# A hybrid decoder layer on one core: seven instead of six of the sixteen contraction pairs in seven block products, and the bias rows stored 32 times per head in the second pass

## The chip, the core and the metric

The kernel runs on one core of one Trainium2 chip. The metric is the device time of one execution, in microseconds (us); a shorter time is better. The engines are TensorE (PE, matmuls; its weight loads are the row PEld), VectorE (DVE), ScalarE (ACT), GpSimd (POOL, idle here) and SyncE (SP), whose queue issues every DMA of this kernel.

## What is computed

The input x has 256 tokens of width 4096. All numbers are float32.

```python
u    = rmsnorm(x, norm_gain)                       # per token
proj = u @ w_in                                    # 4096 x 16384
q, k, v, z_a, hc, b_gate, c_gate, z_c = split(proj, 8)          # 2048 columns each
attn = causal_attention(q, k, v, bias=T5_buckets(rel_bias)) * silu(z_a)   # 16 heads x 128
conv = b_gate * short_conv(c_gate * hc, conv_w) * silu(z_c)     # 3 taps along the tokens
h    = x + concatenate([attn, conv]) @ w_out       # 4096 x 4096
out  = rmsnorm(h, final_gain)
```

With 256 tokens and blocks of 256 the block-sparse attention is plain causal attention within one block. The bias of a query and a key depends on the head and on their distance alone.

## The kernel before, in words

**Passes, quads and units.** The two projections are cut into 20 passes. A pass makes two blocks of 512 output columns for both halves (128 each) of the tokens, so it has four sums of [128, 512]. Passes 0 to 15 are the input projection, passes 16 to 19 the output projection. Passes 0, 2, 4, 6 end in q and k of a group of four heads (`qk_end`), passes 1, 3, 5, 7 in v and z of that group (`vz_end`), passes 8 to 15 in the convolution's inputs (`hc_end`, `zb_end`).

The contraction over 4096 goes in 16 pairs of two tiles of 128. What one pass does with one pair is a quad: one weight load `raw` of [128, 2048] (1 MB), three buffers deep. A quad of an ordinary pair is 8 block products in two units of four. A quad of a pair in `SEVEN` is 7 block products after the Strassen-Winograd pattern, in three units of 3, 2 and 2: they need sums of weight blocks (`sum`, L461 to L463, on DVE) and sums of activation blocks (`c`, `sums_of`, L113), and their products are shared by several of the four outputs. A pass therefore keeps eight PSUM banks, b1 to b8, as accumulators. Banks 1, 5, 6 and 7 belong to the seven products alone and are done with the last `SEVEN` quad of the pass; banks 2, 3, 4 and 8 go on to the end.

A block product is three matmuls of 512 columns (L529, L530, L531): every operand is split into a high part `hi` (a cast on ACT, L472) and the rest `lo` (a subtraction on DVE, L473), and high x high, low x high and high x low are added. `hi` and `lo` have three buffers each, a buffer holding one unit, and `split(u + 2)` stands ahead of the products of unit u. So DVE and ACT can be at most three units ahead of PE. The load of quad n + 2 is issued when the first unit of quad n is split.

**What lies beside it.** In pass 0 the activations are loaded per pair (`xr`, 256 KB), scaled by the gain and split once for all passes: `x_parts`, which for a `SEVEN` pair has 4 sums (L113), a cast of 896 columns (L116) and a subtraction of 896 columns (L117), and else two activations (L137) and two subtractions (L138). Pass 0 also loads x again (`xq`, 8 x 512 KB) for the sum of squares per token (`squares`, L155) and makes the bias rows: a matmul of the table with a one-hot matrix gives one row of 384 values per head, and L195 writes it 128 times per head into DRAM (`bias_d`). A head's bias tile `bt` [128, 384] is read back with a row step of 383 elements, so each partition sees the row one place further on; that takes two DMAs, of 128 KB (L206) and 64 KB (L208). `bias_load(h + 2)` is called in `scores(h)`, after the addition that frees its buffer (L226).

The attention and the convolution are tasks placed among the block products behind the last `SEVEN` quad of a pass (`tasks_of`, L477): `turn`, `scores` and `probs` of four heads in passes 1, 3, 5, 7; `values` and `mixed` in passes 2, 4, 6, 8; `conv` in passes 10, 12, 14 and, from its start, in pass 16. They use banks 1, 5, 6 and 7. `early` (L310) first reads those banks into `e`, with four additions of [128, 512] on DVE; `two_done` (L325) adds the other four banks after the pass's last product. In passes 16 to 19 `out_early` and `out_end` do the same with the residual. In passes 15 and 16 `m_parts` (L146) splits the new operands for the output projection, as `x_parts` does.

**What sets the order.** `ORDERS` gives the pair of each quad of a pass: `FIRST` in pass 0, `OUT_FIRST` in pass 16, and 0, 1, 2, ... in the others. The numbers in `tasks_of` count block products behind the last `SEVEN` quad. The framework then orders each engine's instructions and puts in the waits. SP's queue is in order, and its DMAs report on eight semaphores, DMAHW0 to DMAHW7, in turn, so that a DMA waits until the one eight places before it has landed.

Of the kernel before, what the change touches and what calls it, by code (L numbers as in the profile page):

```python
# [17 lines left out]
P = 128  # L18
# [16 lines left out]
BUCKETS = 32  # L35

# [11 lines left out]
SEVEN = frozenset((0, 2, 4, 6, 8, 10))  # L48
FIRST = (1, 3, 5, 7, 0, 9, 2, 11, 4, 13, 6, 12, 8, 14, 10, 15)
# [10 lines left out]
def hymba_layer(ctx: ExitStack, tc: tile.TileContext, xT, xres, gain, w, convw, wout,  # L60
# [17 lines left out]
    bias_d = dram.tile([H, P, 384], F32, name="bias_d")  # L78
# [76 lines left out]
    def squares(p):  # L155
        for t in range(2):
            xq = pool.tile([P, 2, B], F32, name="xq", tag="vz"[t])
            xq = xq.rearrange("p n c -> p (n c)")
            nc.sync.dma_start(xq, xres[p][:, t * 2 * B:(t + 1) * 2 * B])
            nc.scalar.activation(xq, xq, AF.Square, accum_out=sx[:, t, p:p + 1])  # L160
# [23 lines left out]
    def bias_rows():  # L184
# [10 lines left out]
        nc.sync.dma_start(bias_d, row[:, None, :].to_broadcast([H, P, 384]))  # L195
# [4 lines left out]
    def bias_load(h):  # L200
        if h >= H:
            return
        bt = BT[h] = pool.tile([P, 384], F32, name="bt", bufs=2)

        base = bias_d.offset + h * P * 384
        nc.sync.dma_start(bt[:, :S], bass.AP(tensor=bias_d.tensor, offset=base + 127,  # L206
                                             ap=[[383, P], [1, S]]))
        nc.sync.dma_start(bt[:, S:], bass.AP(tensor=bias_d.tensor, offset=base + 255,  # L208
                                             ap=[[383, P], [1, P]]))
# [125 lines left out]
    def vz_end(g):  # L335
        V[g], Z[g] = (pool.tile([P, 2, B], F32, name=x) for x in "vz")
        two_done((V[g], Z[g]), (rT, rT))
        nc.scalar.activation(Z[g], Z[g], AF.Silu)
# [138 lines left out]
    def tasks_of(p):  # L477
# [5 lines left out]
        if p < 8 and p % 2:  # L483
            for j, (at, banks) in enumerate(zip(((6, 10, 18), (9, 13, 21), (15, 19, 27), (18, 22, 30)),
                                                ((1, 7, 5), (6, 1, 7), (5, 6, 1), (7, 5, 6)))):
                for f, a_, n in zip((turn, scores, probs), at, banks):
                    put(a_, f, p // 2 * HG + j, n)
        elif 2 <= p <= 8:
            for j, (at, banks) in enumerate(zip(((6, 10), (10, 14), (14, 18), (18, 22)),
# [3 lines left out]
        elif p in (10, 12, 14):  # L493
            for j in range(4):
                put(6 + 4 * j, conv, (p - 10) // 2 * 4 + j, (1, 6, 7, 5)[j])
# [38 lines left out]
    for u, (n, kind, at, products) in enumerate(units):  # L534
# [129 lines left out]
```

## Time and profile before

| | |
|---|---|
| median of 3 runs | 1776.4 us (1776.03 to 1777.66) |
| profiled execution, its own time | 1777.55 us |
| its span | 1775.8 us |
| mean granted TensorE clock | 0.989 |
| PE busy | 1723.9 us, 97% of the span, 7698 matmuls |
| DVE busy | 1458.5 us, 82% |
| ACT busy | 1010.4 us, 57% |
| DMA | 370.5 MB, mean 209 GB/s |

All further numbers come from this one execution. Its page gives sums over the whole span; `windows` rows give, for a stretch of time, the busy time of each engine with the count of its instructions in brackets, then the granted clock, the busy share of the DMA engines and GB/s. Rows of groups give the number of instructions, their busy time together, and the mean of one in ns. Neighbouring instructions of DVE overlap a little, so a sum of means is somewhat above the busy time. The times at which passes and quads begin, in us from the start of the span, are the starts of their first matmuls.

### The profile page before, as it was taken

What the parts mean: (1) busy time and instruction counts of PE and PEld (TensorE: products, weight loads), DVE (VectorE), ACT (ScalarE), POOL (GpSimd) and SP (SyncE); (2) the same over time, 40 slices, a digit from 0 to 9 for tenths busy, and PEclk for the clock granted to TensorE, in tenths of its full rate; (3) what the DMA queues carried; (4) which work ended last, traced back from release to release, by engine and by line L of the source; (5) the groups of instructions that cost most, each with busy time, mean ns of one, the idle gap of its engine ahead of it and who ended that gap; (6) DMA issues with size and microseconds to landing.
All of it is one profiled execution on the core that took longest, in us unless ns stands there. A gap on an engine that the chain in (4) does not pass through costs nothing.

```text
span 1775.8 us, 20607 instructions
## 1 busy us (share of the span) xinstructions
PE 1723.9 (97%) x7698; PEld 1414.8 (80%) x7698; DVE 1458.5 (82%) x1591; ACT 1010.4 (57%) x1104; POOL 0.7 (0%) x6
## 2 busy tenths in 40 slices
PE   9489999999999999999999999999999999999996
PEld 7368888888888888888888888888888888788885
DVE  7498787878787878787878887887889999888886
ACT  6375665566556555755555564655555655555553
POOL 0000000000000000000000000000000000000000
PEclk9799999999999999999999999999999999999998
DMA  7875555555555555555645555555555776555563
GB/s 233 233 268 200 206 191 201 191 206 191 200 200 197 199 194 213 174 214 194 223 183 206 203 212 195 213 197 212 194 213 216 260 275 255 201 212 202 193 224 152
DMA packets 65264, 370.53 MB, mean 209 GB/s; under 512 B 7275, under 2 KB 13452, under 8 KB 24460
## 3 DMA queue, kind: packets, MB, share of 16 engines
q1 hardware_dynamic: 65164, 369.22, 58.0%
q8 instruction: 60, 0.98, 0.2%
q14 instruction: 40, 0.33, 0.1%
HBM read 357.66 MB, written 11.53 MB: 208 GB/s over the span
## 4 chain that ended last, share of the span: by engine, by line
PE 93%; DVE 2%; DMA 2%; ACT 1%; issue 1%; SPq 0%; DVEq 0%; ACTq 0%
PE p L531 30%; PE p L529 30%; PE p L530 30%; DMA raw<-in_w_dram 2%; DVE lo L473 1%; ACT hi L472 1%; PE p L216 0%; DMA xq<-in_xres_dram 0%; PE p L223 0%; PE p L240 0%; DVE hg L402 0%; ACT xq L160 0%; DVE hg L414 0%; PE p L251 0%; PE p L250 0%
## 5 line engine op out<-in xcount | busy, mean ns | idle before, releaser
L529 PE MATMUL p<-hi,k 128*128 128x512 f32 x2440 | 958.3, 394 | 32.1 <-ACT hi L472 31.7
L530 PE MATMUL p<-hi,k 128*128 128x512 f32 x2440 | 951.2, 390 | 0.0
L531 PE MATMUL p<-lo,k 128*128 128x512 f32 x2440 | 945.0, 391 | 3.8 <-DVE lo L473 3.3
L473 DVE TENSOR_TENSOR lo<-raw,hi 128x1024 fp32r<-128x1024 f32 (+2 forms) x524 | 692.0, 1333 | 138.5 <-ACT hi L472 137.0
L472 ACT CAST hi<-raw 128x1024 fp32r<-128x1024 f32 (+2 forms) x524 | 596.1, 1145 | 290.3 <-PE p L530 241.9
L529 PEld LDWEIGHTS p<-hi,k 128*128 128x128 f32 x2440 | 459.3, 188 | 132.1 <-ACT hi L472 38.7
L531 PEld LDWEIGHTS p<-lo,k 128*128 128x128 f32 x2440 | 458.2, 188 | 106.5 <-DVE lo L473 9.0
L530 PEld LDWEIGHTS p<-hi,k 128*128 128x128 f32 x2440 | 459.5, 188 | 93.6 <-issue 0.6
L472 ACT CAST hi<-sum 128x1024 fp32r<-128x1024 f32 x240 | 252.9, 1054 | 377.1 <-PE p L530 233.7
L473 DVE TENSOR_TENSOR lo<-sum,hi 128x1024 fp32r<-128x1024 f32 x240 | 292.7, 1219 | 105.7 <-ACT hi L472 105.4
L461 DVE TENSOR_TENSOR sum<-raw 128x1024 f32<-128x1024 f32 x120 | 146.3, 1219 | 6.4 <-DMA raw<-in_w_dram 4.6
L462 DVE TENSOR_TENSOR sum<-sum,raw 128x512 f32<-128x512 f32 x120 | 82.0, 683 | 0.3
L463 DVE TENSOR_TENSOR sum<-sum,raw 128x512 f32<-128x512 f32 x120 | 81.8, 682 | 0.1
L580 ACT ACTIVATE e<-e,rT 128x512 f32<-128x512 f32 x56 | 37.8, 715 | 2.0 <-DVE e L314 1.4
L138 DVE SCALAR_TENSOR_TENSOR k<-xr,g_sb,k 128x256 fp32r<-128x256 f32 x20 | 9.0, 479 | 26.1 <-ACT k L137 26.1
L137 ACT ACTIVATE k<-xr,g_sb 128x256 fp32r<-128x256 f32 x20 | 9.2, 500 | 25.4 <-DMA xr<-in_xT_dram 23.7
L116 ACT CAST k<-c 128x896 fp32r<-128x896 f32 (+1 forms) x22 | 17.3, 796 | 7.9 <-PE p L531 5.0
L117 DVE TENSOR_TENSOR k<-c,k 128x896 fp32r<-128x896 f32 (+1 forms) x22 | 19.7, 902 | 2.4 <-ACT k L116 2.4
L301 DVE SCALAR_TENSOR_TENSOR y<-p,cw,y 128x255 f32<-128x255 f32 (+1 forms) x32 | 15.4, 480 | 4.7 <-ACT y L299 4.3
L226 DVE TENSOR_TENSOR lg<-p,bt 128x384 f32<-128x384 f32 x16 | 8.9, 555 | 12.3 <-PE p L224 12.3
L231 ACT ACTIVATE lg<-lg,st 128x256 f32<-128x256 f32 (+1 forms) x32 | 14.3, 448 | 5.8 <-DVE st L230 5.5
L299 ACT ACTIVATE y<-p,cw 128x256 f32<-128x256 f32 x16 | 7.5, 470 | 12.0 <-PE p L297 12.0
(101 smaller groups left out, 425.5 us busy)
## 6 DMA issues: line engine op xcount, KB each, us to landing
raw<-in_w_dram SPq DMA_DIRECT2D x254, 1024.0 KB, 4.8
raw<-in_wout_dram SPq DMA_DIRECT2D x64, 1024.0 KB, 4.8
xr<-in_xT_dram SPq DMA_DIRECT2D x16, 256.0 KB, 7.8
xq<-in_xres_dram SPq DMA_DIRECT2D x8, 512.0 KB, 6.3
c<-m_d SPq DMA_DIRECT2D x16, 256.0 KB, 3.3
hg<-in_xres_dram SPq DMA_DIRECT2D x4, 1024.0 KB, 7.7
bias_d<-row SPq DMA_DIRECT2D x1, 3072.0 KB, 33.4
out_dram<-hg SPq DMA_DIRECT2D x6, 512.0 KB, 4.0
```

What stands on the lines that cost most here:

```text
L116: nc.scalar.copy(dst[:, :, 0], c)
L117: nc.vector.tensor_tensor(dst[:, :, 1], c, dst[:, :, 0].bitcast(F32), ALU.subtract)
L301: nc.vector.scalar_tensor_tensor(y[:, i:], ps[:, :S - i], cw[:, k, 2 - i:3 - i], y[:, i:], op0=ALU.mult, op1=ALU.add)
L461: nc.vector.tensor_tensor(t[:, :2], raw[:, 1:3], raw[:, :1].to_broadcast([P, 2, B]), ALU.add)
L462: nc.vector.tensor_tensor(t[:, 2], t[:, 0], raw[:, 2], ALU.add)
L463: nc.vector.tensor_tensor(t[:, 3], t[:, 2], raw[:, 3], ALU.add)
L472: nc.scalar.copy(hi[:, c], src[:, c])
L473: nc.vector.tensor_tensor(lo[:, c], src[:, c], hi[:, c].bitcast(F32), ALU.subtract)
L529: nc.tensor.matmul(acc[b_], a, h_, start=s0, stop=False)
L530: nc.tensor.matmul(acc[b_], b, h_, start=False, stop=False)
L531: nc.tensor.matmul(acc[b_], a, l_, start=False, stop=s1)
L580: nc.scalar.activation(es[name], es[name], AF.Copy, scale=rows[c][:, t:t + 1])
```

## The change

Pair 12 joins `SEVEN`. The order of the pairs in pass 0 is another: the first `SEVEN` quad is the third quad, not the fifth. In `OUT_FIRST`, which stays as it was, pair 12 stands between 8 and 10, so that three `SEVEN` quads follow each other. The tasks are placed closer, since only three quads (24 block products) are left behind the last `SEVEN` quad of a usual pass instead of five (40). The bias rows are made in quad 0 of pass 0 instead of quad 2, written 32 instead of 128 times per head, and stored later; a bias tile is then read in eight DMAs (four bands of 32 partitions, 32 KB and 16 KB each) instead of two. The squares take one half-load per quad in quads 4 to 11 instead of two per quad in quads 6 to 9, into other buffers; v and z share buffers with q and k.

```diff
+COPIES = 32
-SEVEN = frozenset((0, 2, 4, 6, 8, 10))
-FIRST = (1, 3, 5, 7, 0, 9, 2, 11, 4, 13, 6, 12, 8, 14, 10, 15)
+SEVEN = frozenset((0, 2, 4, 6, 8, 10, 12))
+FIRST = (1, 3, 0, 5, 2, 7, 4, 9, 6, 11, 8, 13, 10, 14, 12, 15)
...
-    bias_d = dram.tile([H, P, 384], F32, name="bias_d")
+    bias_d = dram.tile([H, COPIES, 384], F32, name="bias_d")
...
-    def squares(p):
-        for t in range(2):
-            xq = pool.tile([P, 2, B], F32, name="xq", tag="vz"[t])
...
+    def squares(n):
+        p, t = divmod(n, 2)
+        xq = pool.tile([P, 2, B], F32, name="xq", tag="qk"[t]).rearrange("p n c -> p (n c)")
+        nc.sync.dma_start(xq, xres[p][:, t * 2 * B:(t + 1) * 2 * B])
+        nc.scalar.activation(xq, xq, AF.Square, accum_out=sx[:, t, p:p + 1])
...
-        nc.sync.dma_start(bias_d, row[:, None, :].to_broadcast([H, P, 384]))
+        return row
+
+    def bias_store(row):
+        nc.sync.dma_start(bias_d, row[:, None, :].to_broadcast([H, COPIES, 384]))
...
-        base = bias_d.offset + h * P * 384
-        nc.sync.dma_start(bt[:, :S], bass.AP(tensor=bias_d.tensor, offset=base + 127,
-                                             ap=[[383, P], [1, S]]))
-        nc.sync.dma_start(bt[:, S:], bass.AP(tensor=bias_d.tensor, offset=base + 255,
-                                             ap=[[383, P], [1, P]]))
+        base = bias_d.offset + h * COPIES * 384
+        for a in range(0, P, COPIES):
+            for c0, c1, at in ((0, S, P - 1), (S, 384, S - 1)):
+                nc.sync.dma_start(bt[a:a + COPIES, c0:c1],
+                                  bass.AP(tensor=bias_d.tensor, offset=base + at - a,
+                                          ap=[[383, COPIES], [1, c1 - c0]]))
...
-        V[g], Z[g] = (pool.tile([P, 2, B], F32, name=x) for x in "vz")
+        V[g], Z[g] = (pool.tile([P, 2, B], F32, name=x, tag=y) for x, y in ("vq", "zk"))
...
-            for j, (at, banks) in enumerate(zip(((6, 10, 18), (9, 13, 21), (15, 19, 27), (18, 22, 30)),
+            for j, (at, banks) in enumerate(zip(((4, 7, 14), (6, 10, 17), (9, 13, 20), (12, 16, 23)),
...
-                put(6 + 4 * j, conv, (p - 10) // 2 * 4 + j, (1, 6, 7, 5)[j])
+                put(4 + 5 * j, conv, (p - 10) // 2 * 4 + j, (1, 6, 7, 5)[j])
...
-            if 6 <= i < 6 + NDP:
-                squares(i - 6)
-            if i == 2:
-                bias_rows()
-            if i == 11:
+            if 4 <= i < 4 + 2 * NDP:
+                squares(i - 4)
+            if i == 0:
+                row = bias_rows()
+            if i == 12:
                 token_scale()
-                bias_load(0)
-                bias_load(1)
+        if p == 1 and i in (0, 4, 5):
+            if i:
+                bias_load(i - 4)
+            else:
+                bias_store(row)
```

What the change moves shows best in the order of the instructions. SP's queue in pass 0, before: the store of the bias rows stands between the weight loads of quad 6 and quad 7 (quads counted from 0).

```order
17 L435 DMA raw<-in_w_dram 128x2048
18 L195 DMA bias_d<-row 2048x1x384
19 L121 DMA xr<-in_xT_dram 128x512
20 L435 DMA raw<-in_w_dram 128x2048
21 L121 DMA xr<-in_xT_dram 128x512
22 L435 DMA raw<-in_w_dram 128x2048
```

The same queue of the changed kernel, around its store: row 41 is the weight load of quad 14 of pass 0, and the first of the five loads behind the store that of quad 15.

```order
41 L439 DMA raw<-in_w_dram 128x2048
42 L122 DMA xr<-in_xT_dram 128x512
43 L198 DMA bias_d<-row 512x1x384
44 L439 DMA raw<-in_w_dram 128x2048 x5
45 L211 DMA bt<-bias_d 32x256
46 L211 DMA bt<-bias_d 32x128
```

The store has moved from behind the seventh weight load to behind the fifteenth and has a quarter of its size, and the first bias tiles are read five weight loads later, with the load of quad 3 of pass 1 ahead of them.

SP's queue at the end of pass 1, before: the bias tiles of four heads (two DMAs each) are read between the weight loads.

```order
67 L206 DMA bt<-bias_d 128x256
68 L208 DMA bt<-bias_d 128x128
69 L435 DMA raw<-in_w_dram 128x2048
70 L206 DMA bt<-bias_d 128x256
71 L208 DMA bt<-bias_d 128x128
72 L435 DMA raw<-in_w_dram 128x2048 x14
```

The same place of the changed kernel, the last eight of 32 bias DMAs in an unbroken row, with their waits: the first row begins the fourth head's tile, and the row L439 is the weight load of quad 2 of pass 2.

```order
107 L211 DMA bt<-bias_d 32x256 [waits DMAHW5_49,DVE_49]
108 L211 DMA bt<-bias_d 32x128 [waits DMAHW6_49]
109 L211 DMA bt<-bias_d 32x256 [waits DMAHW7_49]
110 L211 DMA bt<-bias_d 32x128 [waits DMAHW0_49]
111 L211 DMA bt<-bias_d 32x256 [waits DMAHW1_49]
112 L211 DMA bt<-bias_d 32x128 [waits DMAHW2_49]
113 L211 DMA bt<-bias_d 32x256 [waits DMAHW3_49]
114 L211 DMA bt<-bias_d 32x128 [waits DMAHW4_49]
115 L439 DMA raw<-in_w_dram 128x2048 [waits DMAHW5_49,Activation_49]
```

Before, two weight loads (of quads 0 and 1 of pass 2) stand between the tiles of the four heads; now both are ahead of them, no load is between them, and the load of quad 2 also waits, on DMAHW5, until the first piece of the last tile has landed.

DVE's queue in pass 16, the last quads up to pair 10, before: the rows are the quad of pair 12 (two `lo` of 1024 columns) and the quad of pair 10 (three additions, a `lo` of 1536 and two of 1024).

```order
1122 L461 TENSOR_TENSOR sum<-raw 128x1024
1123 L473 TENSOR_TENSOR lo<-raw,hi 128x1024 x2
1124 L462 TENSOR_TENSOR sum<-sum,raw 128x512
1125 L473 TENSOR_TENSOR lo<-raw,hi 128x1536
1126 L463 TENSOR_TENSOR sum<-sum,raw 128x512
1127 L473 TENSOR_TENSOR lo<-sum,hi 128x1024 x2
```

And of the changed kernel, the quads of pairs 12 and 10:

```order
1184 L465 TENSOR_TENSOR sum<-raw 128x1024
1185 L477 TENSOR_TENSOR lo<-raw,hi 128x1536
1186 L466 TENSOR_TENSOR sum<-sum,raw 128x512
1187 L477 TENSOR_TENSOR lo<-sum,hi 128x1024
1188 L467 TENSOR_TENSOR sum<-sum,raw 128x512
1189 L477 TENSOR_TENSOR lo<-sum,hi 128x1024
1190 L465 TENSOR_TENSOR sum<-raw 128x1024
1191 L477 TENSOR_TENSOR lo<-raw,hi 128x1536
1192 L466 TENSOR_TENSOR sum<-sum,raw 128x512
1193 L477 TENSOR_TENSOR lo<-sum,hi 128x1024
1194 L467 TENSOR_TENSOR sum<-sum,raw 128x512
```

Pair 12's two subtractions have become three additions and three subtractions, and the quad ahead of them, of pair 8, is of the same kind.

More of the change, by code (lines that the diff above doesn't have):

```diff
@@ L152, in m_parts @@
             parts(dst, c[:, :4])
-    def squares(p):
-        for t in range(2):
-            xq = pool.tile([P, 2, B], F32, name="xq", tag="vz"[t])
-            xq = xq.rearrange("p n c -> p (n c)")
-            nc.sync.dma_start(xq, xres[p][:, t * 2 * B:(t + 1) * 2 * B])
-            nc.scalar.activation(xq, xq, AF.Square, accum_out=sx[:, t, p:p + 1])
+    def squares(n):
[3 more added lines that the diff above has]
+        nc.scalar.activation(xq, xq, AF.Square, accum_out=sx[:, t, p:p + 1])
     def rsqrt(dst, ps, n):
@@ L483, in tasks_of @@
         if p < 8 and p % 2:
-            for j, (at, banks) in enumerate(zip(((6, 10, 18), (9, 13, 21), (15, 19, 27), (18, 22, 30)),
-                                                ((1, 7, 5), (6, 1, 7), (5, 6, 1), (7, 5, 6)))):
+            for j, (at, banks) in enumerate(zip(((4, 7, 14), (6, 10, 17), (9, 13, 20), (12, 16, 23)),
+                                                ((1, 7, 5), (6, 1, 6), (5, 7, 7), (6, 1, 5)))):
                 for f, a_, n in zip((turn, scores, probs), at, banks):
@@ L488, in tasks_of @@
         elif 2 <= p <= 8:
-            for j, (at, banks) in enumerate(zip(((6, 10), (10, 14), (14, 18), (18, 22)),
+            for j, (at, banks) in enumerate(zip(((4, 8), (8, 12), (12, 16), (16, 20)),
                                                 ((1, 7), (6, 5), (1, 7), (6, 5)))):
```

## The prediction

> **What bounds the kernel now.** I read the page's first two parts, then stretches of pass 0, the weight loads on SP's queue, and then the ends of the passes. First the span, the engines, and PE and its granted clock in 40 slices of 44 us:
>
> ```profile
> span 1775.8 us, 20607 instructions
> PE 1723.9 (97%) x7698; PEld 1414.8 (80%) x7698; DVE 1458.5 (82%) x1591; ACT 1010.4 (57%) x1104; POOL 0.7 (0%) x6
> PE   9489999999999999999999999999999999999996
> PEclk9799999999999999999999999999999999999998
> ```
>
> PE is full from the fourth slice to the last but one; the one hole lies in the second. How fast PE runs when full, in pass 9, which has no tasks (only the matmuls of L530, a third of a pass, are counted):
>
> ```profile
> 835.00:918.00 83.00, 47.46 (x122) 22.90 (x123) 1.00 0.56 203
> ```
>
> 3 x 122 = 366 matmuls in 83.0 us are 0.2268 us each: 4.76 us for a quad of 21, 5.44 us for one of 24. That sets most of the span. Stretches of the beginning (us, PE, PEld, DVE, ACT, POOL busy, clock, DMA share, GB/s); quad 1 of pass 1 begins at 136.0:
>
> ```profile
> 0.00:6.10 6.10, 3.59 (x8) 1.03 (x8) 1.17 (x4) 3.00 (x5) 0.70 (x6) 1.00 0.51 168
> 6.10:28.90 22.80, 22.76 (x94) 18.75 (x95) 17.07 (x26) 15.35 (x23) 0.00 (x0) 1.00 0.94 361
> 28.90:70.00 41.10, 16.63 (x71) 12.60 (x70) 16.37 (x22) 10.30 (x14) 0.00 (x0) 0.76 0.80 130
> 70.00:136.00 66.00, 58.29 (x226) 43.29 (x227) 60.73 (x85) 51.63 (x71) 0.00 (x0) 0.94 0.76 280
> ```
>
> In the third row PE stands still for 24.5 of 41.1 us and the DMAs move 130 GB/s. In the fourth DVE is busy for 60.7 of 66.0 us. What the hole is, from SP's queue, the chain that ended last and the DMA issues (KB each, us to landing):
>
> ```profile
> 32.07 0.69 SPq L195 DMA_DIRECT2D bias_d<-row  x1
> 42.66 4.32 SPq L435 DMA_DIRECT2D raw<-in_w_dram  x1
> ```
> ```profile
> 42.66 26.78 DMA raw<-in_w_dram
> 69.53 1.05 ACT hi L472
> ```
> ```profile
> raw<-in_w_dram SPq DMA_DIRECT2D x254, 1024.0 KB, 4.8
> bias_d<-row SPq DMA_DIRECT2D x1, 3072.0 KB, 33.4
> bt<-bias_d SPq DMA_DIRECT2D x16, 128.0 KB, 2.1
> bt<-bias_d SPq DMA_DIRECT2D x16, 64.0 KB, 1.9
> ```
>
> The bias store takes 33.4 us; the weight load issued 10.6 us behind it lands after 26.8 us instead of 4.8. So the kernel is bound by PE except in pass 0, which waits first for this store and then for DVE.
>
> **The change part by part.** DVE's work by form over the whole run, and one row of ACT (count, busy us, mean ns, idle before):
>
> ```profile
> L473 DVE TENSOR_TENSOR lo<-raw,hi 128x1024 fp32r<-128x1024 f32 x396 | 476.5, 1219 | 104.0 <-ACT hi L472 102.6
> L473 DVE TENSOR_TENSOR lo<-sum,hi 128x1024 fp32r<-128x1024 f32 x240 | 292.7, 1219 | 105.7 <-ACT hi L472 105.4
> L473 DVE TENSOR_TENSOR lo<-raw,hi 128x1536 fp32r<-128x1536 f32 x120 | 210.1, 1751 | 32.0 <-ACT hi L472 32.0
> L461 DVE TENSOR_TENSOR sum<-raw 128x1024 f32<-128x1024 f32 x120 | 146.3, 1219 | 6.4 <-DMA raw<-in_w_dram 4.6 <-DMA raw<-in_wout_dram 0.5
> L462 DVE TENSOR_TENSOR sum<-sum,raw 128x512 f32<-128x512 f32 x120 | 82.0, 683 | 0.3
> L463 DVE TENSOR_TENSOR sum<-sum,raw 128x512 f32<-128x512 f32 x120 | 81.8, 682 | 0.1
> L117 DVE TENSOR_TENSOR k<-c,k 128x896 fp32r<-128x896 f32 x12 | 13.0, 1084 | 2.4 <-ACT k L116 2.4
> L113 DVE TENSOR_TENSOR c<-c 128x128 f32<-128x128 f32 x48 | 12.1, 283 | 2.2 <-DMA c<-m_d 1.1 <-ACT c L129 0.9
> L138 DVE SCALAR_TENSOR_TENSOR k<-xr,g_sb,k 128x256 fp32r<-128x256 f32 x20 | 9.0, 479 | 26.1 <-ACT k L137 26.1
> L472 ACT CAST hi<-sum 128x1024 fp32r<-128x1024 f32 x240 | 252.9, 1054 | 377.1 <-PE p L530 233.7
> ```
>
> *Matmuls.* One block product less per pass, 3 x 0.2268 = 0.68 us; in passes 1 to 19 that is 12.9 us off PE's path. (Pass 0 is counted apart.)
>
> *DVE's price.* A quad of seven costs DVE 1.219 + 0.683 + 0.682 + 1.751 + 2 x 1.219 = 6.77 us, an ordinary one 2 x 1.219 = 2.44. That is 4.33 more per pass, 87 in all, so about 1540 of 1750 us. A pair of quads, one of each kind, takes 9.2 us of DVE under 10.2 of PE: hidden where they alternate. If the cover were gone, it would cost 4.33 - 0.68 per pass and more.
>
> *Pass 0.* The hole: the store has a quarter of the bytes, so by its own rate 33.4 / 4 = 8.4 us, and it now stands behind the load of quad 14. The load of quad 15 follows one quad of DVE work later and is needed only after DVE has done quads 13 and 14, some 12 us on; with 4.8 us of landing that leaves 7 for what remains of the 8.4. I cost it at nothing, with 8.4 as its upper end. What is late next is DVE. Up to 136 us it was busy 1.17 + 17.07 + 16.37 + 60.73 = 95.3. The added quad brings 6.77 + 4 x 0.283 + 1.084 against 2.44 + 2 x 0.479: 5.6, some 5.3 after overlaps, so 100.6. Its idle time remains: 4.9 before 6.1 us; in the second row it was 5.7, now with the first quad of seven third instead of fifth about 3; in the last row 5.3 in half a pass, where the squares' loads came in pairs. With them spread I take 5 for all the rest. 100.6 + 13 = 113.6 instead of 136: **22.5 us gained**. The floor, without the 5, is 108.5 (27.5 gained); if every later stretch idles as the last row does, 5.3 per 66 us, 5 becomes 8, and with half of the store's 8.4 on top it is about 121 (15 gained). The squares, the earlier bias matmul and the shared buffers add no work; their buffers are last read before their next writers' pass ends, so I add no wait.
>
> *The ends of the passes.* Rows before: the end of pass 3 (attention), the beginning of pass 4, the end of pass 10 (convolution), pass 16 up to its last quad of seven, its end, and the first three quads of pass 17:
>
> ```profile
> 363.00:396.20 33.20, 33.20 (x165) 27.67 (x164) 23.23 (x36) 22.15 (x40) 0.00 (x0) 1.00 0.56 189
> 396.20:415.00 18.80, 18.80 (x84) 15.58 (x83) 18.23 (x19) 13.41 (x12) 0.00 (x0) 1.00 0.48 181
> 973.80:1002.90 29.10, 29.10 (x137) 24.09 (x136) 24.01 (x32) 15.14 (x19) 0.00 (x0) 1.00 0.57 208
> 1423.10:1497.00 73.90, 73.74 (x328) 60.53 (x329) 67.29 (x76) 42.53 (x43) 0.00 (x0) 1.00 0.76 285
> 1497.00:1507.80 10.80, 10.80 (x49) 8.95 (x48) 10.80 (x14) 4.56 (x4) 0.00 (x0) 1.00 0.57 194
> 1507.80:1525.70 17.90, 16.27 (x67) 11.86 (x66) 16.44 (x20) 12.01 (x18) 0.00 (x0) 1.00 0.50 169
> ```
>
> The tasks keep their work but lose two ordinary quads around them: 2 x 5.44 = 10.9 us of PE, 4 x 1.219 = 4.9 of DVE, 4 x 1.054 = 4.2 of ACT. The end of pass 3 becomes 22.3 us with DVE 18.4 and ACT 18; that of pass 10 becomes 18.2 with DVE 19.1. After the last product DVE must still add four banks before the next pass goes on, and it is full there already (18.23 of 18.80) without PE waiting. Any backlog carried in shows on PE. DVE may be three units ahead, which covers most of this. Where nothing is carried in, a seam costs 0 (the second row); where it is, up to 2.9, the measured 17.9 - 66 x 0.2268 of the last row. I take 0.5 for the four ends with attention and the three with convolution (3.5), and 0.15 for the other ten (1.5).
>
> Pass 16: up to its last quad of seven DVE has 67.29 + 4.3 + 1.5 (the larger `m_parts` of pair 12, 4 x 0.283 + 1.084 against a subtraction of 512, 0.683) = 73.1 under 73.2 of PE, and the last three quads in a row are of seven: 3 x 6.77 = 20.3 under 14.3. The lead of three units covers about half of that 6: 3 us (0 to 6). Then `out_early` finds DVE full (10.80 of 10.80), and the 2.9 at the beginning of pass 17 grow, by 1.5 (0 to 2.9). Losses together 3.5 + 1.5 + 3 + 1.5 = **9.5** (2 to 26).
>
> *The bias tiles.* SP's issues and landings before:
>
> ```profile
> 196.13 0.33 SPq L206 DMA_DIRECT2D bt<-bias_d  x1
> 196.50 0.43 SPq L208 DMA_DIRECT2D bt<-bias_d  x1
> 198.86 0.32 SPq L206 DMA_DIRECT2D bt<-bias_d  x1
> ```
>
> A head's tile now takes 8 x 0.38 = 3 us of SP instead of 0.8. The load of quad 2 of the next pass stands behind all four tiles. The fourth head's scores stand behind product 16 of 24, 8 x 0.68 = 5.4 us before the pass ends, and their addition, by my estimate, behind one cast and one subtraction (2.3 us) that wait in the queues ahead of it: some 3 us before the end. 3 us of issues and the landing of a first piece put that load about 1 us past the end, and its landing 4.8 later, while PE comes to quad 2 at 4.76 + 5.44 = 10.2. Taking off 3.2 for its cast and subtraction leaves a margin of 1 us: nothing, at worst 2 us in each of four passes, held by the range of the seams. The Trainium skill speaks against this part ("DMA: Bandwidth & Descriptors", Rules for kernel authors: transfers under 64 KB should be coalesced, and two transfers to disjoint partition halves serialize). Here the pieces are 32 and 16 KB; by its rule the sum would be that of the slow rival below.
>
> The sum: 1777.55 (the profiled execution's own time, 1.75 above its span) - 22.5 - 12.9 + 9.5 = 1751.65. The median of the three runs is 1.15 below that execution, so **1750.5**.
>
> **The rivals.** *The store is still felt* (8.4 us hidden by nothing): 1759. For it: before, weight loads behind the store stood still. Against: then three times the load time was missing, now there are 7 us to hide in. *The seams each lose as pass 16 to 17 does*: nine of them (four, three, and both sides of pass 16) at 2.9 is 26, with 3 in pass 16, 29 in all: 1776.4 - 22.5 - 12.9 + 29 = 1770. For it: the demand of 105% at the convolution; against: passes 3 and 10 lost nothing. *DVE runs without a gap in pass 0 and the seams cost nothing*: 1776.4 - 27.5 - 12.9 = 1736. *Slower: the pieces land one after another*, 1.9 us each as the 64 KB row shows. (It is the rule of the Trainium skill named above.) Then 32 take 61 us, from about 15 us before an odd pass ends to 46 behind it; the load of quad 2, which may go out 2.7 behind it, is 43 late in passes 1, 3 and 5, and 13 in pass 7 with 16 pieces: 142 us, 1750 + 142 = 1892. It decides from 0.55 us per piece (17.6 us of room / 32), and is slower than before from 0.8. Against: the second DMA of a tile goes out 0.37 us behind the first and lands 1.9 us after its own issue; one after the other it would be 3.6. So here the trace disagrees with serial landing, though for two pieces, not eight. That the product isn't saved can't be: the order has 60 matmuls less.
>
> **How the numbers follow.** The forecast 0.60, the store 0.12, the seams 0.13, without losses 0.10, the serial pieces 0.05. The range, 1738 to 1766, takes the ends of pass 0 (-5, +7.5) and the losses up to 18, and leaves out parts of the last three. A measurement of this kernel can tell about 0.2%, 3.5 us, from no change. Faster by more: 0.93; within: 0.02; slower: 0.05.
>
> **What would show it.** Right: no idle stretch of PE above 5 us in pass 0, quad 1 of pass 1 begins near 113 with DVE above 90% ahead of it, a usual pass without tasks takes 82.3 us, and weight loads keep landing in about 5 us through the ends of odd passes. Wrong: PE waiting for `raw` at quad 15 or at quad 2 of passes 2, 4, 6, 8, or losses of 2 us and more at each seam, would make the time higher; PE above 95% in pass 0 would make it lower.

## The result and the profile after

The changed kernel takes **1750.42 us** (median of 4 runs, 1750.24 to 1751.39), where the kernel before, on the same chip, takes 1777.03 (4 runs, 1776.03 to 1778.91): a ratio of 0.985, with a 95% interval of 0.9833 to 0.9867. The forecast was 1750.5 in a range of 1738 to 1766. The profiled execution took 1750.47 us, with a span of 1748.4, which is 27.4 less than before. Of the two runs of e1 below, one took 2485 us at a granted clock of 0.654 and is left out.

The page of the changed kernel: the span, the engines, PE and its granted clock in 40 slices.

```profile
span 1748.4 us, 20772 instructions
PE 1715.6 (98%) x7638; PEld 1402.8 (80%) x7638; DVE 1533.4 (88%) x1678; ACT 1035.3 (59%) x1125; POOL 0.7 (0%) x6
PE   9989999999999999999999999999999999999996
PEclk9989999999999999999999999999999999999998
```

The hole of the second slice is gone; the third slice, in which pass 0 ends, has an 8. DVE has gone from 1458.5 to 1533.4 us (the working said about 1540). The beginning in stretches (us, PE, PEld, DVE, ACT, POOL busy, clock, DMA share, GB/s); quad 1 of pass 1 begins at 113.3, where it began at 136.0 before:

```profile
0.00:6.40 6.40, 3.21 (x8) 1.04 (x8) 1.17 (x4) 3.00 (x5) 0.70 (x6) 1.00 0.54 160
6.40:29.00 22.60, 22.35 (x88) 17.24 (x89) 20.40 (x32) 16.56 (x25) 0.00 (x0) 0.92 0.89 327
29.00:80.00 51.00, 49.83 (x208) 37.74 (x207) 51.00 (x68) 44.53 (x63) 0.00 (x0) 1.00 0.88 320
80.00:94.00 14.00, 12.34 (x47) 9.44 (x46) 12.25 (x24) 7.47 (x10) 0.00 (x0) 0.88 0.79 244
94.00:113.30 19.30, 14.34 (x50) 10.76 (x49) 15.32 (x18) 10.29 (x12) 0.00 (x0) 0.82 0.36 120
```

From 29 to 80 us DVE has no idle moment, while PE's 208 matmuls, at the 0.2275 us of pass 9 below, are 47.3 of the 51 us. So pass 0 reads as bound by DVE there, as the working had it; no run takes work off DVE alone to show it. DVE is busy 1.17 + 20.40 + 51.00 + 12.25 + 15.32 = 100.1 us in all. But the last stretch isn't DVE's: PE stands still for 5 of its 19.3 us, and the clock is at 0.82.

That stretch on ACT (start, duration, operation, idle time before it and what ended it): L587 are the four scalings of the sums `e`, two of which are shown, and the last row begins the casts of quad 15, the last of pass 0.

```profile
90.95 1.05 ACT L476 CAST hi<-sum 128x1024 fp32r<-128x1024 f32 x1
95.31 0.72 ACT L587 ACTIVATE e<-e,rQ 128x512 f32<-128x512 f32 x1 [3.31 <-DVE e L318]
96.70 0.72 ACT L587 ACTIVATE e<-e,rT 128x512 f32<-128x512 f32 x1 [0.67 <-DVE e L320]
...
98.56 3.35 ACT L476 CAST hi<-raw 128x1024 fp32r<-128x1024 f32 x3
```

ACT idles for 3.3 us in front of a scaling, since that waits for DVE's additions, and these wait for PE's last product of seven. The casts stand behind the scalings in ACT's queue, and PE waits for the casts:

```profile
99.64 0.79 PE L533 MATMUL p<-hi,k 128*128 128x512 f32 x1 [4.92 <-ACT hi L476]
...
101.49 0.63 PE L533 MATMUL p<-hi,k 128*128 128x512 f32 x1
101.91 0.63 PE L534 MATMUL p<-hi,k 128*128 128x512 f32 x1
```

After the 4.92 us the matmuls start 0.42 us apart instead of 0.23, until 106.2. That is most of what brings the clock of this stretch to 0.82, and by my estimate (15 matmuls, 0.2 us each) it costs some 3 us more.

SP's queue around the store and around the bias pieces at the end of pass 3 (which ends at 371.7), and the landings (count, KB each, median us):

```profile
72.58 0.69 SPq L198 DMA_DIRECT2D bias_d<-row  x1
77.37 29.55 SPq L439 DMA_DIRECT2D raw<-in_w_dram  x5
...
357.56 14.82 SPq L211 DMA_DIRECT2D bt<-bias_d  x32
372.48 15.48 SPq L439 DMA_DIRECT2D raw<-in_w_dram  x5
```
```profile
raw<-in_w_dram SPq DMA_DIRECT2D x254, 1024.0 KB, 4.8
bt<-bias_d SPq DMA_DIRECT2D x64, 32.0 KB, 1.8
bt<-bias_d SPq DMA_DIRECT2D x64, 16.0 KB, 1.8
```

The 32 pieces of four heads take 14.82 us of SP, 0.46 us each without a gap: the scores' additions of the four heads end at 357.53, 360.25, 363.88 and 368.27 us, each before SP comes to its tile. The load behind them goes out 0.8 us past the end of the pass (the working said about 1), the pieces land in 1.8 us each (the larger ones before in 2.1 and 1.9), and the weight loads still in 4.8 at the median. The store is felt by the load directly behind it, that of quad 15:

```profile
raw<-in_w_dram SPq DMA_DIRECT2D x1, 1024.0 KB, 10.5
```

It lands at 87.9 us, 10.5 after its issue instead of 4.8, and its casts begin at 98.56, so nothing waits for it. Then the end of pass 3, pass 9 (the matmuls of L534 alone), and passes 16 and 17:

```profile
349.40:371.70 22.30, 22.30 (x118) 18.62 (x116) 18.76 (x32) 17.71 (x36) 0.00 (x0) 1.00 0.44 127
```
```profile
807.00:889.60 82.60, 47.10 (x121) 22.72 (x121) 1.00 0.56 205
```
```profile
1390.10:1481.50 91.40, 87.40 (x380) 68.44 (x379) 85.53 (x104) 50.13 (x50) 0.00 (x0) 1.00 0.71 260
1481.50:1567.70 86.20, 83.60 (x364) 67.59 (x363) 78.36 (x81) 48.44 (x52) 0.00 (x0) 1.00 0.58 204
```

The end with attention shows no wait of PE. Pass 16 is the other way: it took 84.7 us before and takes 91.4 now, although it has a product less. PE idles for 4.0 us of it; a matmul's record lasts 0.39 us and the next begins 0.23 behind it, so that shorter delays show as no idle time. DVE is busy for 85.53. The waits from 1390 to 1490 us (total, times, longest):

```profile
ACT hi L476 <- DVE sum L467: 19.7, 8, 3.0
PEld p L533 <- ACT hi L476: 7.3, 8, 1.5
```

ACT's casts wait for DVE's third addition, and PE waits for the casts: the lead over PE is used up, and DVE's work holds PE there.

### The profile page after: what moved, and what is told of

It reads as the page before. It is cut to its first block, busy times and chain, and to the rows that moved or that the text cites. A ratio compares the mean times of both kernels' runs of the same rounds, so it can differ in the third digit from the quotient of the medians.

```text
span 1748.4 us, 20772 instructions
## 1 busy us (share of the span) xinstructions
PE 1715.6 (98%) x7638; PEld 1402.8 (80%) x7638; DVE 1533.4 (88%) x1678; ACT 1035.3 (59%) x1125; POOL 0.7 (0%) x6
## 4 chain that ended last, share of the span: by engine, by line
PE 90%; DVE 7%; issue 1%; ACT 1%; DMA 0%; SPq 0%; DVEq 0%; ACTq 0%
PE p L535 29%; PE p L533 29%; PE p L534 29%; DVE lo L477 3%; ACT hi L476 1%; DVE sum L465 1%; DVE sum L466 1%; DVE k L118 0%; DVE sum L467 0%; PE p L220 0%; PE p L227 0%; DVE c L114 0%; PE p L244 0%; DVE hg L400 0%; DVE hg L406 0%
## 5 line engine op out<-in xcount | busy, mean ns | idle before, releaser
L534 PE MATMUL p<-hi,k 128*128 128x512 f32 x2420 | 945.2, 391 | 0.5 <-DVE k L118 0.3
L535 PE MATMUL p<-lo,k 128*128 128x512 f32 x2420 | 930.8, 392 | 2.5 <-DVE lo L477 2.3
L477 DVE TENSOR_TENSOR lo<-raw,hi 128x1024 fp32r<-128x1024 f32 (+2 forms) x504 | 675.9, 1359 | 42.4 <-ACT hi L476 41.2
L476 ACT CAST hi<-raw 128x1024 fp32r<-128x1024 f32 (+2 forms) x504 | 581.6, 1165 | 209.0 <-PE p L534 173.1
L476 ACT CAST hi<-sum 128x1024 fp32r<-128x1024 f32 x280 | 295.0, 1053 | 444.5 <-PE p L534 244.8
L533 PEld LDWEIGHTS p<-hi,k 128*128 128x128 f32 x2420 | 455.1, 188 | 115.4 <-ACT hi L476 19.2
L534 PEld LDWEIGHTS p<-hi,k 128*128 128x128 f32 x2420 | 456.4, 189 | 93.9 <-DVE k L118 3.1
L477 DVE TENSOR_TENSOR lo<-sum,hi 128x1024 fp32r<-128x1024 f32 x280 | 341.9, 1221 | 135.3 <-ACT hi L476 135.1
L465 DVE TENSOR_TENSOR sum<-raw 128x1024 f32<-128x1024 f32 x140 | 170.9, 1221 | 8.6 <-DMA raw<-in_w_dram 6.3
L467 DVE TENSOR_TENSOR sum<-sum,raw 128x512 f32<-128x512 f32 x140 | 95.9, 685 | 0.2
L466 DVE TENSOR_TENSOR sum<-sum,raw 128x512 f32<-128x512 f32 x140 | 95.8, 684 | 0.2
L587 ACT ACTIVATE e<-e,rT 128x512 f32<-128x512 f32 x56 | 37.8, 716 | 0.7 <-DVE e L320 0.7
L114 DVE TENSOR_TENSOR c<-c 128x128 f32<-128x128 f32 x56 | 14.3, 282 | 0.1
L402 ACT ACTIVATE e<-hg 128x512 f32<-128x512 f32 x16 | 10.0, 625 | 6.9 <-DVE hg L400 6.6
```

What stands on the lines that cost most here:

```text
L465: nc.vector.tensor_tensor(t[:, :2], raw[:, 1:3], raw[:, :1].to_broadcast([P, 2, B]), ALU.add)
L466: nc.vector.tensor_tensor(t[:, 2], t[:, 0], raw[:, 2], ALU.add)
L467: nc.vector.tensor_tensor(t[:, 3], t[:, 2], raw[:, 3], ALU.add)
L476: nc.scalar.copy(hi[:, c], src[:, c])
L477: nc.vector.tensor_tensor(lo[:, c], src[:, c], hi[:, c].bitcast(F32), ALU.subtract)
L533: nc.tensor.matmul(acc[b_], a, h_, start=s0, stop=False)
```

## The experiments

The result alone doesn't tell these theories apart. Mine: the gain is pass 0 (its hole gone, DVE next), less what DVE loses in pass 16. The rivals: the place of the store rather than its size, losses that come from other work, and a price of the small DMAs. Each run was timed beside the kernel before on its chip (1777.59, 1777.76 and 1777.65 us in the three groups e1 to e4, e5 to e8 and e9 to e11). Single profiles of the end of pass 0 differ by more than medians do: quads 14 and 15 take 21.1 us in the changed kernel's profile, and 18.5 in e6's and 19.2 in e9's, which have the same pass 0. So gains there are taken from the medians, and the profiles show only who waits for whom.

**e1: the bias part alone** (the kernel before, with six pairs and its own order of pairs):

```diff
+COPIES = 32
...
-                bias_rows()
+                row = bias_rows()
...
-                bias_load(0)
-                bias_load(1)
+        if p == 1 and i in (0, 4, 5):
+            if i:
+                bias_load(i - 4)
+            else:
+                bias_store(row)
```

> The kernel before with only the bias part of the change: 32 copies, the later store, eight DMAs per tile. Pair 12 stays an ordinary pair, the order of pass 0 stays. My theory: nearly the whole gain is pass 0. Without the store's hole, DVE's 95.3 us of work up to quad 1 of pass 1 and some 15 us of idle time put that quad at 111 us instead of 136, and the rest is as before: about 1752 us. Rival: the sum's two terms are about equal (the hole is only partly worth what the trace shows, since something else waits next), and this part alone gives 1763.

Measured: 1753.68 us, one run, so there is no interval. Quad 1 of pass 1 begins at 111.5. So the bias part alone brings 24 of the 27 us, and the rest of the change, the seventh pair above all, 3.3 on top of it. The theory holds.

**e2: the seventh pair alone** (the changed kernel with 128 copies, stored in quad 5 of pass 0, and two DMAs per bias tile, the first two tiles read in pass 0, as before), of which the diff shows the store's part:

```diff
-COPIES = 32
+COPIES = 128
...
+            if i == 5:
+                bias_store(row)
```

> The changed kernel with 128 copies again, stored in the middle of pass 0, and two DMAs per tile: the sevens and the dense tasks alone. My theory: the hole of 25 us stays, the saved matmuls (13 us) are nearly eaten by DVE in pass 0 and by pass 16: about 1774 us. Rival: the saved matmuls come through whole: 1764.

Measured: 1770.04 us (1767.63 to 1771.97; ratio 0.9955, 0.9936 to 0.9975), between the two. Alone, this part gains 7.6 us, more than the 3.3 that it adds to the bias part. SP's queue, and what ACT waits for:

```profile
39.22 0.70 SPq L198 DMA_DIRECT2D bias_d<-row  x1
39.96 11.29 SPq L122 DMA_DIRECT2D xr<-in_xT_dram  x1
```
```profile
ACT k L138 <- DMA xr<-in_xT_dram: 19.8, 1, 19.8
```

The hole is there again, behind a store that takes 35.6 us. Here the first to be late is an `xr` of 256 KB, not a weight load.

**e3: 128 copies at the late place** (the changed kernel with one number changed):

```diff
-COPIES = 32
+COPIES = 128
```

> The changed kernel with 128 copies at the new, late place (two DMAs of 16 partitions become one band: the tile is read in two DMAs). It tells size from place. My theory: both count. The store of 33 us begins at 72.6 us, the load of quad 15 is issued at 77.4 behind it and needed at 98.6, so it comes about 10 us late: 1760 us. Rival: the late place hides it whatever its size: 1750.

Measured: 1764.52 us (2 runs; ratio 0.9922, 0.9893 to 0.9951). At the end of pass 0:

```profile
PE p L533 <- ACT hi L476: 17.9, 1, 17.9
ACT hi L476 <- DMA raw<-in_w_dram: 13.4, 2, 12.9
```

The theory's mechanism is there: the load of quad 15 comes late, by 12.9 us instead of the 10 that gave 1760. The late place is 5.5 us better than e2's (both read a tile in two DMAs), but a store of 128 copies is felt at both. The size counts for more: 14.1 us at the late place.

**e4: 32 copies at the early place** (the changed kernel, with the store in quad 5 of pass 0):

```diff
+            if i == 5:
+                bias_store(row)
...
-        if p == 1 and i in (0, 4, 5):
-            if i:
-                bias_load(i - 4)
-            else:
-                bias_store(row)
+        if p == 1 and i in (4, 5):
+            bias_load(i - 4)
```

> The changed kernel with its small store in the middle of pass 0, behind the weight load of quad 8, in place of the end of pass 0. My theory: 8.4 us of store are within what the loads can wait in pass 0, since DVE and not the loads sets its pace: 1750 to 1752 us. Rival: the place is what hides it, and here it costs what it takes: 1758.

Measured: **1744.64 us** (2 runs, 1744.54 and 1744.73; ratio 0.981, 0.9782 to 0.9839), faster than either theory had it. A store of 768 KB makes no hole in the middle of pass 0 either, though it takes 11.1 us, more than the 8.4 of the working:

```profile
bias_d<-row SPq DMA_DIRECT2D x1, 768.0 KB, 11.1
```

The further 5.8 us come from the end of pass 0, where quads 13, 14 and 15 take 6.89, 8.21 and 5.44 us (6.94, 12.18 and 8.88 in the changed kernel; of these 7.5 us, 1.9 are lost again ahead of quad 13 and in the first quad of pass 1). ACT's queue there is ordered in another way. Some rows of each queue, first of the changed kernel:

```
64 L476 CAST hi<-sum 128x1024
65 L587 ACTIVATE e_876<-e_876,rQ 128x512
66 L587 ACTIVATE e_877<-e_877,rT 128x512
67 L587 ACTIVATE e_878<-e_878,rQ 128x512
68 L587 ACTIVATE e_879<-e_879,rT 128x512
69 L476 CAST hi<-raw 128x1024 x2
```

And with the early store:

```
66 L317 COPY e_877<-p_250 128x512
67 L476 CAST hi<-raw 128x1024 x2
68 L476 CAST hi<-raw 128x1536
69 L476 CAST hi<-sum 128x1024
70 L586 ACTIVATE e_877<-e_877,rQ 128x512
71 L476 CAST hi<-sum 128x1024
```

The casts of quad 15 now stand ahead of the scalings, and DVE does that quad's subtractions (the first row) ahead of the additions for `e`:

```profile
95.83 2.36 DVE L477 TENSOR_TENSOR lo<-raw,hi 128x1024 fp32r<-128x1024 f32 x2 [0.90 <-ACT hi L476]
98.11 0.68 DVE L318 TENSOR_TENSOR e<-p,e 128x512 f32<-128x512 f32 x1
```

That the framework orders ACT so because the late store stands ahead of quad 15's load is likely, but was only argued. Whether the order is what costs the time is the next run.

**e5: ACT's order alone** (the changed kernel with the scalings of pass 0 taken from ahead of the last casts to behind the pass's end):

```diff
-                for _, t, c, name in ENDS:
-                    nc.scalar.activation(es[name], es[name], AF.Copy, scale=rows[c][:, t:t + 1])
+                if p:
+                    scaled(es, rows)
...
+        if g == 0:
+            for b_, t, n, name in ENDS:
+                dst = (Q[g], K[g])[n][:, t]
+                nc.vector.tensor_tensor(dst, cur["acc"][b_], cur["es"][name], ALU.add)
+                nc.scalar.activation(dst, dst, AF.Copy, scale=(rQ, rT)[n][:, t:t + 1])
+            return
```

> The changed kernel with one difference in pass 0: the four sums e are not scaled ahead of the pass's last additions; the additions of the last product are plain ones on DVE, and ACT scales q and k behind them. ACT's queue then holds the casts of the last quad directly behind the last quad of seven, where the changed kernel has four scalings ahead of them. Theory (the scalings, which wait for DVE's additions, hold the casts and so PE): the wait of PE of 4.9 us ahead of the last quad's first product goes, quad 1 of pass 1 begins near 108 instead of 113.3, and the time is 1745 (1743 to 1747). Rival (the end of pass 0 is held by DVE's work, and the queue order of ACT only shows it): quad 1 of pass 1 begins at 112 or later, 1749 to 1751. In the kernel with the early store of 32 copies, which gained 5.8, both could have been the cause.

Measured: 1746.98 us (1745.75 to 1748.67; ratio 0.9828, 0.9814 to 0.9843): 3.4 us gained, at the upper edge of what the theory said (against e6, with the pass 0 of the changed kernel on the same chip, it is 2.7, and the runs of the two overlap). The profiled run was the slowest of the four; its quad 1 of pass 1 begins at 111.5, not near 108. Of that, 1.5 us come from the first quad of pass 0, which began 0.35 us later and ran longer at half the clock. Quads 14 and 15 together take 17.8 us instead of 21.1. One wait of PE went and another came:

```profile
98.90 0.80 PE L541 MATMUL p<-lo,k 128*128 128x512 f32 x1 [3.26 <-DVE lo L483]
```

The casts are in time now, but on DVE the four additions for `e` (94.98 to 97.6) still stand ahead of quad 15's subtractions, which begin at 97.63. So the end of pass 0 is a matter of order on both engines: some 3 us for ACT's part. That the 2.3 us by which e4 is faster still are DVE's part agrees with the two traces, but is not shown: no run changes it alone.

**e6: three quads of seven in a row, or two** (the changed kernel, with pairs 12 and 14 exchanged in pass 16, and the operands made in the old order):

```diff
-OUT_FIRST = (1, 3, 5, 0, 7, 2, 9, 4, 11, 6, 13, 8, 12, 10, 14, 15)
+M_FIRST = (1, 3, 5, 0, 7, 2, 9, 4, 11, 6, 13, 8, 12, 10, 14, 15)
+OUT_FIRST = (1, 3, 5, 0, 7, 2, 9, 4, 11, 6, 13, 8, 14, 10, 12, 15)
```

> The changed kernel with pairs 12 and 14 exchanged in the order of the quads of pass 16, so that two quads of seven stand next to each other (10 and 12) with an ordinary one ahead of them, instead of three in a row; the order in which the new operands are made stays. The last quad of seven is then quad 14 instead of quad 13. Theory (the third quad of seven in a row is what costs 4.6 of the 7.4 us in pass 16): the triple's loss goes, one of up to 2.5 stays for the pair, and the end of the pass with one ordinary quad behind the last of seven costs 0 to 2: 1748 (1746.5 to 1750). Rival (DVE's total in pass 16 sets the loss, wherever the quads stand): pass 16 stays at 91 us, 1750.4.

Measured: 1749.65 us (1747.71 to 1752.29; ratio 0.9848, 0.9831 to 0.9864), no difference that these runs can tell from 1750.42. Passes 16 and 17:

```profile
1387.70:1475.40 87.70, 86.14 (x381) 68.91 (x380) 82.44 (x100) 50.24 (x50) 0.00 (x0) 1.00 0.73 267
1475.40:1565.20 89.80, 85.62 (x365) 68.75 (x364) 81.60 (x85) 48.44 (x53) 0.00 (x0) 0.98 0.56 199
```

The theory was right on pass 16, which is 3.7 us shorter, and wrong on the kernel: pass 17 is 3.6 longer, its first quad 10.24 us instead of 6.05. The backlog was not removed, only handed on. The rival had the place wrong (pass 16 doesn't stay at 91) and the time right: passes 16 and 17 together take 177.5 us instead of 177.6, with DVE's total unchanged (164.0 and 163.9).

**e7: 16 copies, twice the pieces:**

```diff
-COPIES = 32
+COPIES = 16
```

> The changed kernel with 16 instead of 32 copies: a bias tile takes 16 DMAs of 16 and 8 KB instead of 8. The store has half the bytes. Theory (SP's issues are what counts, 0.38 to 0.46 us each, and the load of quad 2 stands behind them): the pieces of a pass end take 25 to 30 us of SP instead of 14.8, the load of quad 2 goes out 11 to 15 us past the pass's end instead of 0.8, and PE waits for it 9 to 13 us in passes 2, 4 and 6: 1778 (1770 to 1790). Rival (the issues are mostly waits for the scores, and there is room left): 1750. A further rival (the pieces land one after another, 1.6 us each): 64 x 1.6 = 102 us per pass end, over 1950.

Measured: 1792.24 us (1789.09 to 1792.67; ratio 1.0078, 1.0063 to 1.0093), slower than the kernel before. SP's queue at the end of pass 3, which ends at 381.8 here, what PE waits for behind it, and the landings:

```profile
367.47 30.94 SPq L211 DMA_DIRECT2D bt<-bias_d  x64
398.51 9.65 SPq L439 DMA_DIRECT2D raw<-in_w_dram  x4
```
```profile
ACT hi L476 <- DMA raw<-in_w_dram: 13.8, 1, 13.8
PE p L533 <- ACT hi L476: 12.1, 2, 11.9
```
```profile
bt<-bias_d SPq DMA_DIRECT2D x32, 16.0 KB, 1.7
bt<-bias_d SPq DMA_DIRECT2D x32, 8.0 KB, 1.7
```

The mechanism is the theory's, and the time 2 us above its range: 64 issues at 0.48 us each, and quad 2's load goes out 16.7 us past the end of the pass. PE waits 12 us for it, within the 9 to 13. Passes 2, 4 and 6 are each 14.5 to 16.1 us longer, since the matmuls of quad 2 run at half the clock after the wait (it takes 7 to 8 us instead of 4.8), which the 1778 had left out. Pass 0 gives some 4 us back: quad 1 of pass 1 begins at 109.0, with half the store and another order on ACT. So with 32 copies some 4 us of room are left (16.7 - 11.9 - 0.8), and with 64 pieces it is gone.

**e8: DVE's additions in pass 0 given to GpSimd** (the changed kernel):

```diff
-    def sums_of(c):
+    def sums_of(c, e=None):
...
-            nc.vector.tensor_tensor(c[:, dst], c[:, a], c[:, b], op)
+            (e or nc.vector).tensor_tensor(c[:, dst], c[:, a], c[:, b], op)
...
-            sums_of(c)
+            sums_of(c, nc.gpsimd)
```

> The changed kernel with the four additions of 128 columns for each of the seven pairs in pass 0 (28 in all, 0.28 us each on DVE) on GpSimd instead of DVE. Theory (pass 0 is bound by DVE, which is busy without a gap from 29 to 80 us): 28 x 0.28 = 7.9 us come off DVE, some of it after overlaps, and pass 0 ends 4 to 8 us sooner: 1745 (1742 to 1747), unless GpSimd's additions, for which the trace has no duration, take longer than the 5 us that a quad of seven leaves. Rival (ACT's queue and the weight loads set pass 0): 1750.

Measured: 1751.65 us (1750.96 to 1752.17; ratio 0.9854, 0.9839 to 0.9868), nothing gained. GpSimd's additions (all of them, then the first two groups of four by time), and one kind of DVE's instructions in this kernel from 6.9 to 80 us:

```profile
L114 POOL TENSOR_TENSOR c<-c 128x128 f32<-128x128 f32 x28 | 24.5, 884 | 61.7 <-ACT c L130 60.5
```
```profile
13.97 1.96 POOL L114 TENSOR_TENSOR c<-c 128x128 f32<-128x128 f32 x4 [12.66 <-ACT c L130]
25.75 6.04 POOL L114 TENSOR_TENSOR c<-c 128x128 f32<-128x128 f32 x4 [9.82 <-ACT c L130]
```
```profile
L139 DVE SCALAR_TENSOR_TENSOR k<-xr,g_sb,k 128x256 fp32r<-128x256 f32 x12 | 7.0, 612 | 0.0
```
```profile
ACT k L117 <- POOL c L114: 13.8, 5, 3.3
```

And the same kind in the changed kernel, from 6.4 to 80 us:

```profile
L139 DVE SCALAR_TENSOR_TENSOR k<-xr,g_sb,k 128x256 fp32r<-128x256 f32 x14 | 6.5, 472 | 0.0
```

An addition takes 0.884 us on GpSimd on average and 0.282 on DVE, so four of them take 2 to 6 us instead of 1.1, and ACT waits 13.8 us for them. DVE's own instruction grows from a mean of 472 to 612 ns: a pair of them beside GpSimd's additions (at 36.41 us) takes 1.28 us, a pair without (at 23.09) 0.87. The run doesn't decide whether pass 0 is bound by DVE: it took work off DVE and put a wait in its place. The Trainium skill ("Perfetto Trace Analysis", Optimizing Scalar/DVE Operations) says that offloading from DVE to GpSimd might not help, since the two share an SBUF read port; this trace agrees (472 to 612 ns, and nothing gained). Another page of the Trainium skill ("GPSIMD Engine Reference", Engine selection) has a two-input operation about 2 times slower on GpSimd. Here it is 1.6 times in the first group (0.46 us each), beside which DVE is all but idle, and 3.1 times on average, with DVE busy beside most of the others.

**e9: the seventh pair only in the input projection** (the changed kernel):

```diff
+SIX = SEVEN - {12}
...
+    def seven(p, q):
+        return q in (SEVEN if p < N_PAIRS else SIX)
...
-        if q in SEVEN:
-            sums_of(c)
+        if q in SIX:
+            sums_of(c)
...
-            if q in SEVEN:
+            if seven(p, q):
```

> The changed kernel with pair 12 as an ordinary pair in the four passes of the output projection (16 to 19), and of seven in the other sixteen; the first part of the program stays. Theory (the seventh pair costs more than it saves there): passes 16 to 19 become as before the change, 84.73 + 86.03 + 83.53 + 98.40 = 352.7 instead of 91.47 + 86.21 + 82.87 + 97.82 = 358.4, so 5.7 us come off although 12 matmuls more than 2.7 us worth are back: 1744.7 (1743 to 1746.5). Rival (the loss comes from passes 15 and 16 being full of DVE's other work, the operands and the convolution, and stays): 2.7 us are lost, 1753.

Measured: 1744.71 us (1743.62 to 1745.74; ratio 0.9814, 0.98 to 0.9827), the theory's number. Pass 16:

```profile
1389.60:1476.00 86.40, 85.38 (x383) 69.91 (x382) 81.37 (x97) 48.59 (x49) 0.00 (x0) 1.00 0.75 275
```

In the trace passes 16 to 19 take 354.4 us instead of 358.4, so 4.0 of the 5.7 us between the medians lie there; the profiled run is the slowest of the four, and pass 16 keeps 1.7 us over its 84.73 of before. So the loss is mostly, not wholly, the seventh pair's, and the exact number is in part luck. Twelve matmuls (2.7 us) come back and the kernel is faster: in the output projection the seventh pair costs more than it saves.

**e10: e4 and e9 together:**

> The kernel with the early store of 32 copies (1744.64) and, as well, pair 12 as an ordinary pair in passes 16 to 19. Theory (the two gains lie in different stages and add): 1744.6 - 5.7 = 1739 (1737 to 1741). Rival (the loss in pass 16 isn't the seventh pair's): 1747.

Measured: **1740.26 us** (1740.05 to 1740.76; ratio 0.9789, 0.9776 to 0.9803). It lies in the theory's range: the gains add, and this kernel beats both the one before and the changed one, by 37.4 and 10.2 us.

**e11: e10 with two ordinary quads at the end of pass 0:**

```diff
-FIRST = (1, 3, 0, 5, 2, 7, 4, 9, 6, 11, 8, 13, 10, 14, 12, 15)
+FIRST = (1, 3, 0, 5, 2, 7, 4, 9, 6, 11, 8, 13, 10, 12, 14, 15)
```

> The kernel of the run before with the last two pairs of pass 0 but one exchanged, so that two ordinary quads instead of one stand behind the last quad of seven. Theory (what PE still waits at the end of pass 0 is the chain of the four sums e between the last quad of seven and the split of the last quad): quads 14 and 15 and the first of pass 1 lose 2 to 4 us less, 1736 (1734 to 1738). Rival (DVE's work alone sets the end of pass 0, wherever the last quad of seven stands): 1739.

Measured: 1741.18 us (1740.36 to 1741.93; ratio 0.9794, 0.9781 to 0.9807). The theory falls. Quad 14, now an ordinary one, is shorter (6.02 us instead of 6.62) and quad 15 stays at 5.44, but quads 12 and 13, now two of seven in a row, take 8.10 and 7.22 instead of 6.07 and 6.87. So the loss moves with the dense place, as the rival has it, by which DVE's work sets the end of pass 0.

## Why the prediction was right, point by point

| term | forecast | measured |
|---|---|---|
| pass 0 up to quad 1 of pass 1 | -22.5 | -22.7 (136.0 to 113.3) |
| matmuls of passes 1 to 19 | -12.9 | -12.9 |
| seams with attention, convolution and others | +5.0 | 0.0 |
| pass 16 | +3.0 | +7.4 |
| beginning of pass 17 | +1.5 | +0.9 |
| sum | -25.9 | -27.3 |

*Pass 0.* DVE's sum was right (100.6 forecast, 100.1 measured), and so was its idle time, 13 and 13.2 us. But the 5 taken "for all the rest" don't lie where they were put. The working saw them as disturbances spread over half a pass; DVE has none from 29 to 80 us, and 5.7 us behind that, 4.0 of them in the last stretch, where a queue order makes ACT and PE wait. e4 and e5 show that these can be removed; the floor of 108.5 given for that case is 107.7 in e4. So the number was right and its reason partly wrong: what is late next at the end of pass 0 is the chain of the sums `e`, which the working didn't name. That it agrees within 0.2 us is luck: with the same pass 0, quad 1 of pass 1 begins at 110.9 in e6's profile and at 112.9 in e9's. And the sign "DVE above 90% ahead of it" didn't come: DVE is busy for 88% of the 113.3 us; the working's own 100.6 of 113.6 is 89%.

*The store.* "I cost it at nothing" holds: PE never waits for a weight load at quad 15, whose casts wait for the scalings. Its terms were off both ways: the small store takes 10.3 us in e1 and 11.1 in e4, not 8.4, and the load of quad 15 has 21 us from its issue to its casts, not 12. e3 shows that the size was needed for it (14.1 us more with 128 copies), e4 that the late place was not. The hidden price of the place is the order on ACT.

*Matmuls.* 363 matmuls in the 82.60 us of pass 9 are 0.2275 us each. Passes 1 (from its quad 1) to 15, 18 and 19 together are 11.59 us shorter, which is 17 x 0.68 = 11.56.

*The seams.* That agreement leaves nothing for their losses, taken together: passes 3, 5 and 7, which end with attention, are 1.15 us shorter each, those with the convolution about 0.7, the others from 2 to 14 are 0.25 to 0.6 shorter and pass 15 is 1.5. The step "0.5 for the four ends with attention and the three with convolution" was too cautious: three units of lead cover them, as the full row of pass 3's end and the lengths of the passes say, and the rival with 2.9 us at each seam is refuted.

*Pass 16.* The step "the lead of three units covers about half of that 6: 3 us" failed in its size. It treated the three quads in a row as the only debt. The trace has some 4.6 us there (quads 12 and 13 take 6.82 and 7.35 us instead of about 4.76), and some 3 in the first six quads, where the larger operands are made. No lead was left from there, as e6 shows: where the quads stand doesn't matter, only DVE's total. The losses came to 8.3 in all instead of 9.5, because two wrong sizes went against each other: 5.6 too much at the seams and pass 17, 4.4 too little in pass 16. That is luck too.

*The bias pieces.* The 1 us past the end and the landing are as forecast. An issue takes 0.46 us, not 0.38, and SP is full from the first head's scores on instead of waiting for the fourth's, which its issues reach 0.5 us after they are ready. The margin was some 4 us, not 1. (The slow rival's "2.7" would be 2.2 by the same rows, 10.2 - 4.8 - 3.2, and the "8" at the far end of pass 0 about 7, 5.3 per 66 us over 85 to 92; neither changes the forecast.) The slow rival, pieces that land one after another, is refuted by 1.8 us for each of 128 pieces, and e7 with 1.7 us for pieces half that size: there the time goes into SP's issues, not into landings. So the second half of the rule of the Trainium skill quoted in the prediction ("DMA: Bandwidth & Descriptors", Rules for kernel authors: transfers to disjoint partition halves serialize), read as the prediction reads it, doesn't hold here, for pieces this small. Its first half, that transfers under 64 KB pay mostly overhead, agrees with the traces: pieces of 8 KB land in 1.7 us and those of 128 KB in 2.1.

## What to carry to other kernels

Price a small DMA by what stands behind it in its queue: here 32 issues at a pass's end cost nothing and 64 cost 15 us, because one weight load came after them. When a trade of TensorE work for VectorE work is priced, take VectorE's total over each stretch and ask whether a lead is left, since moving the dense place only hands the backlog on; where there is none, the saved product can cost more than it brings. And a moved transfer can change the order of another engine's queue: compare that order before putting a difference down to the transfer itself.

## What the runs showed of the hardware

The clock can fall after short waits, and after the same waits it need not. In e4 two waits of 1.27 and 1.44 us within 3 us, with five matmuls between them, were followed by matmuls 0.43 us apart:

```profile
91.31 1.22 PE L533 MATMUL p<-hi,k 128*128 128x512 f32 x2 [1.44 <-ACT hi L476]
92.33 0.63 PE L534 MATMUL p<-hi,k 128*128 128x512 f32 x1
92.76 0.63 PE L535 MATMUL p<-lo,k 128*128 128x512 f32 x1
```

In e10, whose pass 0 is the same, waits of 1.21 and 1.44 us at the same place were followed by matmuls 0.23 us apart:

```profile
91.42 0.73 PE L537 MATMUL p<-hi,k 128*128 128x512 f32 x2 [1.44 <-ACT hi L480]
91.99 0.39 PE L538 MATMUL p<-hi,k 128*128 128x512 f32 x1
92.22 0.40 PE L539 MATMUL p<-lo,k 128*128 128x512 f32 x1
```

Quad 14 takes 8.21 us in e4 and 6.62 in e10. No run here shows what decides, so a difference of a us or two at such a place can't be read from one profile. The Trainium skill ("TensorE: Matmul & The Clock Gate", Why this matters for your kernels) warns of idle gaps above some 3 us; the 4.92 us of the changed kernel and the 3.26 of e5 agree with that, the pair of short ones in e4 goes below it.

And GpSimd at work lengthened an instruction of DVE from a mean of 472 to 612 ns, as DVE at work lengthened GpSimd's additions (in e8, 0.46 us each beside a DVE that is all but idle, 0.88 on average), which no run had been meant to show.
